# Up projection of the last 1024 tokens as seven products of half blocks, down projection in stages of its own

## The chip, the cores and the metric

The kernel runs on one core of a Trainium2 chip. The metric is device time of one launch in microseconds (us); lower is better. The core has five engines with a queue each: PE multiplies matrices, DVE and ACT work element by element, POOL does small work and issues some DMAs, SP issues most DMAs.

## What is computed

One layer of a hybrid decoder over 2048 tokens of width 1024, float32: a mixer (differential attention, a gated linear recurrence, gated DeltaNet), its output projection and residual, then a gated feed-forward of width 2816 with a causal convolution over three tokens, and a final norm. The part that changes:

```python
h = h + jnp.einsum("bte,ed->btd", mix, w_out[l])

u = rmsnorm(h, ffn_norm_w[l])
up = jnp.einsum("btd,df->btf", u, ffn_w_up[l])
up = causal_depthwise_conv(up, ffn_conv_w[l]) + ffn_conv_b[l].astype(up.dtype)
gate, val = jnp.split(up, 2, axis=-1)
h = h + jnp.einsum("btf,fd->btd", jax.nn.silu(gate) * val, ffn_w_down[l])
return rmsnorm(h, final_norm_w)
```

## The kernel before

Each large product is made of three PE passes: `split` (L89) turns a float32 operand into a high part (a cast on ACT, L92) and a low part (a subtraction on DVE, L93), and `mm3` (L98) adds high x high, high x low and low x high in PSUM, as three matmuls of 128 x 128 by 128 x 512.

`phase_p` projects the input in two halves of 1024 tokens, and runs the recurrences and the attention of the first half beside that. `tail` (L983) does the rest. Its order in the code: the DeltaNet groups of the second half (`dn_half`), then for each 512 tokens (a piece) the output projection and residual (`residual`), the norm with its transposes (`piece_norm`) and the feed-forward (`ffn`). Pieces 0 and 1 run one after the other; beside them the second half's attention (L882) is fed in through `Pump`, a share of its steps after each group. Its memory is that of the DeltaNet groups. Pieces 2 and 3 come last, together, and share each weight load.

`ffn` takes two blocks of 128 features at a time. `ffn_block` loads the gate and the value weights of a block (512 KB each, tile `wu`), splits them, multiplies by the piece's `uh`, `ul` (24 matmuls each), copies PSUM to `raw`, convolves (L1154, L1157) and gates (L1161 to L1163), and splits the gated product into `gh`, `gl`. `down` (L1085) then multiplies the two blocks by their down weights, six matmuls per PSUM bank, and DVE adds each bank to the residual `h` in SBUF (L1098). After the last block `final` scales and stores.

The order on each engine's queue is not that of the code: the code is traced with `tile.TileContext(nc, schedule_with_timeline_sim=True)`, and a planner orders the instructions at build time by their place in the code and when it thinks them ready; buffers of one name and pool are taken in turn, and one that is in use makes its next user wait. A pool that is closed leaves its memory to the next one opened. Each engine then runs its queue in order.

Of the kernel before, what the change touches and what calls it, by code (L numbers as in the profile page):

```python
# [19 lines left out]
P = 128  # L20
# [10 lines left out]
W_BUFS = 3  # L31
D_BUFS = 2
G_BUFS = 3
S_BUFS = 2
T_BUFS = 2
U_BUFS = 1
N_BUFS = 2
# [9 lines left out]
PUMP0 = 0  # L47
PUMP1 = 19
E2_AT = 9
# [34 lines left out]
class K:  # L84
# [13 lines left out]
    def mm3(self, ps, a, b, start, stop):  # L98
        mm = self.nc.tensor.matmul
# [52 lines left out]
    def scratch(self, ctx):  # L152
# [6 lines left out]
        self.s_mix = d.tile([8, P, T], F32, name="s_mix")  # L159

# [290 lines left out]
    def dn_open(self, ctx):  # L451
        tc = self.tc
        self.dw = ctx.enter_context(tc.tile_pool(name="dw", bufs=1))
        self.dps = ctx.enter_context(tc.tile_pool(name="dps", bufs=2, space=PSUM))
# [409 lines left out]
    def att_open(self, ctx, p0_bufs, p1_bufs, s_bufs, t_bufs, slots):  # L864
        tc = self.tc
        self.p_bufs, self.kslots = (p0_bufs, p1_bufs), slots
        self.kq = ctx.enter_context(tc.tile_pool(name="kq", bufs=1))
        self.ap = ctx.enter_context(tc.tile_pool(name="ap", bufs=2))
        self.sm = ctx.enter_context(tc.tile_pool(name="sm", bufs=2))
        self.pss = ctx.enter_context(tc.tile_pool(name="pss", bufs=s_bufs, space=PSUM))  # L870
        self.pst = ctx.enter_context(tc.tile_pool(name="pst", bufs=t_bufs, space=PSUM))
        pso = ctx.enter_context(tc.tile_pool(name="pso", bufs=1, space=PSUM))
# [110 lines left out]
    def tail(self, out):  # L983
        tc, nc, a = self.tc, self.nc, self.a
        with ExitStack() as ctx:
            fc = ctx.enter_context(tc.tile_pool(name="fc", bufs=1))
            self.fw = ctx.enter_context(tc.tile_pool(name="fw", bufs=2))
            self.fps = ctx.enter_context(tc.tile_pool(name="fps", bufs=U_BUFS, space=PSUM))
            self.fpd = ctx.enter_context(tc.tile_pool(name="fpd", bufs=N_BUFS, space=PSUM))
            self.wup = a["ffn_w_up"][0].rearrange("(db p) f -> p db f", p=P)  # L990
            wbc = self.wbc = fc.tile([P, D], F32, name="wbc")
            nc.sync.dma_start(wbc, a["ffn_norm_w"].broadcast_to([P, D]))
            carry = self.carry = fc.tile([P, 2 * NF, 2], F32, name="carry")
            nc.gpsimd.memset(carry, 0.0)
# [229 lines left out]
```

## Time and profile before

| | |
|---|---|
| time, median of 3 runs | 3050.1 us (3049.32 to 3056.87) |
| profiled execution | 3049.23 us, span 3047.5 us |
| PE busy | 2924.1 us, 96% |
| DVE busy | 2087.3 us, 68% |
| ACT busy | 1351.2 us, 44% |
| POOL busy | 315.7 us, 10% |
| mean granted clock of PE | 0.978 |

The span goes from the first to the last instruction of one execution; the rest of its time lies around it. A busy share is the time in which an engine has an instruction under way. PE's instructions overlap each other, so the sum of their durations is longer than its busy time, and a full PE can still be one that waits a little at each matmul. The profile gives the time from the span's start.

### The profile page before, as it was taken

To read this page: it belongs to the slowest core of one execution; us is meant where nothing else is said; L and a number is where in the kernel's file an instruction comes from. 1 tells how busy PE (TensorE), PEld (TensorE's weight loads), DVE (VectorE), ACT (ScalarE), POOL (GpSimd) and SP (SyncE) were. 2 spreads that over 40 slices of the span, in tenths; PEclk is the share of its full clock that TensorE was granted. 3 is DMA by queue.
4 is the path that set the end of the run, shared out by engine and by line. 5 is a ranking of instruction groups with operands and counts; after the bars stand their busy time and mean duration, and the time that the engine had idled before them with its cause. 6 is when DMAs were issued, how large, how long until landed. Compare 5 with 4: busy or idle time off the path is not lost.

```text
span 3047.5 us, 50581 instructions
## 1 busy us (share of the span) xinstructions
PE 2924.1 (96%) x20010; PEld 2384.5 (78%) x20010; DVE 2087.3 (68%) x3923; ACT 1351.2 (44%) x2558; POOL 315.7 (10%) x569
## 2 busy tenths in 40 slices
PE   8999989999998899999899999999799999999998
PEld 6888867777887677877687888887577888888887
DVE  7463775386677877967798888888467555555556
ACT  4222242253455444343666766667235223333323
POOL 1100101021111111202011111110001000000000
PEclk9999979999999999999999999999899999999999
DMA  5336444355646423324524333332313111111111
GB/s 173 94 109 168 129 118 135 91 143 152 183 124 195 103 77 97 90 77 136 158 68 128 100 109 97 101 100 76 100 52 104 49 42 49 56 49 46 52 42 69
DMA packets 373008, 307.88 MB, mean 101 GB/s; under 512 B 65883, under 2 KB 322723, under 8 KB 372771
## 3 DMA queue, kind: packets, MB, share of 16 engines
q1 hardware_dynamic: 333475, 258.51, 28.9%
q0 software_dynamic: 39296, 46.14, 6.2%
q8 instruction: 157, 2.57, 0.4%
q14 instruction: 80, 0.66, 0.1%
HBM read 237.49 MB, written 67.11 MB: 100 GB/s over the span
## 4 chain that ended last, share of the span: by engine, by line
PE 86%; DVE 5%; DMA 3%; ACT 3%; issue 2%; POOL 0%; SPq 0%; POOLq 0%; ACTq 0%; DVEq 0%
PE pp L100 17%; PE pp L101 17%; PE pp L102 17%; PE pd L100 7%; PE pd L102 7%; PE pd L101 7%; PE o L966 4%; PE s L921 4%; PE t L958 2%; PE t L443 1%; PE t L808 1%; DMA wr<-in_ffn_w_down_dram 1%; DVE nb L925 1%; DMA q<-s_q 1%; DMA x<-in_x_dram 1%
## 5 line engine op out<-in xcount | busy, mean ns | idle before, releaser
L100 PE MATMUL pp<-uh,wh 128*128 128x512 f32 x2304 | 916.5, 398 | 12.4 <-ACT raw L1148 9.1
L101 PE MATMUL pp<-ul,wh 128*128 128x512 f32 x2304 | 909.5, 395 | 2.9 <-DVE ul L194 2.9
L102 PE MATMUL pp<-uh,wl 128*128 128x512 f32 x2304 | 906.2, 394 | 0.0
L100 PEld LDWEIGHTS pp<-uh,wh 128*128 128x128 f32 x2304 | 436.2, 189 | 110.7 <-ACT raw L1148 15.4
L101 PEld LDWEIGHTS pp<-ul,wh 128*128 128x128 f32 x2304 | 436.0, 189 | 92.9 <-DVE ul L194 4.6
L102 PEld LDWEIGHTS pp<-uh,wl 128*128 128x128 f32 x2304 | 435.5, 189 | 92.9 <-issue 0.7
L100 PE MATMUL pd<-dh,gh 128*128 128x512 f32 x832 | 332.4, 402 | 15.0 <-ACT gh L92 11.0
L101 PE MATMUL pd<-dl,gh 128*128 128x512 f32 x832 | 329.5, 396 | 0.5 <-DVE dl L93 0.4
L102 PE MATMUL pd<-dh,gl 128*128 128x512 f32 x832 | 324.2, 395 | 0.0
L1098 DVE TENSOR_TENSOR h<-h,pd 128x512 f32<-128x512 f32 x360 | 243.7, 684 | 112.6 <-PE pd L102 111.7
L1157 DVE SCALAR_TENSOR_TENSOR cv<-raw,columns,cv 128x512 f32<-128x512 f32 x352 | 263.9, 750 | 73.7 <-ACT cv L1154 70.0
L927 ACT ACTIVATE p<-s,nb 128x512 f32<-128x512 f32 (+3 forms) x320 | 199.4, 625 | 127.6 <-DVE nb L925 108.7
L925 DVE TENSOR_REDUCE nb<-s 128x1 f32<-128x512 f32 (+3 forms) x320 | 192.5, 608 | 72.2 <-PE s L921 35.8
L93 DVE TENSOR_TENSOR wl<-wu,wh 128x1024 fp32r<-128x1024 f32 x132 | 161.3, 1223 | 71.2 <-ACT wh L92 69.7
L921 PE MATMUL s<-k,q 128*128 128x512 f32 (+3 forms) x640 | 190.3, 388 | 18.3 <-ACT p L927 13.8
L100 PEld LDWEIGHTS pd<-dh,gh 128*128 128x128 f32 x832 | 157.2, 190 | 51.1 <-ACT gh L92 11.5
L92 ACT CAST wh<-wu 128x1024 fp32r<-128x1024 f32 x132 | 138.7, 1051 | 127.2 <-PE pp L101 115.4
L92 ACT CAST gh<-th 128x512 fp32r<-128x512 f32 x120 | 74.1, 619 | 256.6 <-DVE th L1163 182.0
L101 PEld LDWEIGHTS pd<-dl,gh 128*128 128x128 f32 x832 | 157.8, 190 | 34.6 <-DVE dl L93 1.9
L102 PEld LDWEIGHTS pd<-dh,gl 128*128 128x128 f32 x832 | 157.0, 189 | 35.1 <-DVE gl L93 0.4
L92 ACT CAST dh<-wr 128x1024 fp32r<-128x1024 f32 x78 | 80.2, 1051 | 234.9 <-PE pd L102 210.8
L1154 ACT ACTIVATE cv<-raw,columns 128x512 f32<-128x512 f32 x176 | 144.1, 819 | 13.0 <-POOL raw L1149 0.4
(281 smaller groups left out, 4186.5 us busy)
## 6 DMA issues: line engine op xcount, KB each, us to landing
wu<-in_ffn_w_up_dram SPq DMA_DIRECT2D x132, 512.0 KB, 4.0
wr<-in_ffn_w_down_dram SPq DMA_DIRECT2D x66, 512.0 KB, 3.3
wr<-in_w_in_dram SPq DMA_DIRECT2D x56, 512.0 KB, 4.4
q<-s_q POOLq DMA_DIRECT2D x32, 512.0 KB, 5.7
k<-s_k POOLq DMA_DIRECT2D x28, 512.0 KB, 5.4
v<-s_v POOLq DMA_DIRECT2D x28, 512.0 KB, 5.1
wr<-in_w_out_dram SPq DMA_DIRECT2D x24, 512.0 KB, 4.9
x<-in_x_dram SPq DMA_DIRECT2D x16, 512.0 KB, 5.1
```

The lines of the kernel that those rows point to most:

```text
L92: self.nc.scalar.copy(hi, src)
L93: self.nc.vector.tensor_tensor(lo, src, hi.bitcast(F32), op=ALU.subtract)
L100: mm(ps, lhsT=a[0], rhs=b[0], start=start, stop=False)
L101: mm(ps, lhsT=a[0], rhs=b[1], start=False, stop=False)
L102: mm(ps, lhsT=a[1], rhs=b[0], start=False, stop=stop)
L921: nc.tensor.matmul(ps[:, 0:n], lhsT=qS[:, m, i, qs], rhs=kS[c][:, m, 0:n], start=i == 0, stop=i == 1 and not diag)
L925: nc.vector.tensor_reduce(nb[:, c, m:m + 1], ps[:, 0:n], axis=AX.X, op=ALU.max, negate=True)
L927: nc.scalar.activation(t, ps[:, 0:n], AF.Exp, bias=nb[:, c, m:m + 1], accum_out=ls[:, c, m:m + 1])
L966: nc.tensor.matmul(oc[:, 0:256], lhsT=x[:, ks], rhs=vt, start=c == 0 and k == 0 and i == 0, stop=c == len(pd) - 1 and ks.stop == n and i == 1)
L1098: nc.vector.tensor_tensor(h, h, pt, op=ALU.add)
L1154: nc.scalar.activation(c, r[:, 0:512], AF.Identity, bias=self.fcb[:, idx:idx + 1], scale=self.fcw_l[0][:, idx:idx + 1])
L1157: nc.vector.scalar_tensor_tensor(c, r[:, j:j + 512], self.fcw_l[j][:, idx:idx + 1], c, op0=mult, op1=ALU.add)
```

## The change

Pieces 0 and 1 are now normed one after the other and then go through each feature block together, so that a weight block is loaded and split once for both. The gated products aren't split there but written to DRAM (`s_g`), and the residual goes to DRAM too (`s_h`). The down projection is a stage of its own for each 512 tokens and each 512 outputs: its weights and the gated products are loaded and split block by block, all 22 blocks are summed in four PSUM banks, and DVE adds the residual once at the end. The attention of the second half starts after 20 of the 44 block steps and ends with the third of these stages; of its two PSUM banks for transposes one is left, and the feed-forward has four banks in place of three.

For the last 1024 tokens the up projection is a product of 2 x 2 blocks: gate and value by two halves of the 1024 inputs, times two halves of the inputs by two pieces. `forms` makes the seven sums of input blocks in SBUF once, `up7` makes the sums of weight blocks (two on POOL, two on DVE) for each feature block and then seven products where eight stood, adding them up in PSUM and on DVE. A pair of pieces has one convolution and gating of 1024 columns. Their down projection is again four stages, after all up products.

```diff
-T_BUFS = 2
+T_BUFS = 1
+DOWN_LAST = 4
+ATT_AT = 20
...
+        self.s_h = d.tile([T, D], F32, name="s_h")
+        self.s_g = d.tile([NF, P, T], F32, name="s_g")
...
     def tail(self, out):
...
+            main = self.ups = self.dns = Rot((pool(ctx, "fps", bufs=4, space=PSUM), "pp"))
+            ca = ExitStack()
+            with ExitStack() as c1:
+                ux = pool(c1, "ux", bufs=1)
+                self.fw = pool(c1, "fw", bufs=2)
+                with ExitStack() as c2:
+                    self.dn_open(c2, side="right")
+                    self.ct = self.load_consts(self.dw, DN_CONSTS, "dn_consts")
+                    rs = pool(c2, "rs", "right", bufs=1)
+                    self.dn_half(1)
+                    u = []
+                    for s in range(2):
+                        h = [x for i in range(2) for x in rows(slot(ux, 4 + i, F32) if s == 0 else slot(rs, i, F32))]
+                        self.residual([s], [h], rs, 3, 2)
+                        us = [[slot(ux, s * 4 + x * 2 + g) for g in range(2)] for x in range(2)]
+                        self.piece_norm(h, lambda g, cs, pv: self.hi_lo(us[0][g][:, :, cs], us[1][g][:, :, cs], pv))
+                        u.append(us)
+                self.att_open(ca, P0_BUFS, P1_BUFS, S_BUFS, T_BUFS, 4, side="right")
+                att = Pump(self.attention(8, 16), 4 * 100)
+                pump = lambda n: att.upto((n - ATT_AT) / (2 * NF + 3 * 11 - ATT_AT))
+                for f in range(NF):
+                    for s in self.ffn_block(f, u):
+                        pump(2 * f + s + 1)
+            with ExitStack() as c1:
+                self.fw = pool(c1, "fw2", bufs=2)
+                down = self.down([0, 1], out, 1, main)
+                for s, dc, f in down:
+                    n = 2 * s + dc
+                    if n < 3:
+                        pump(2 * NF + n * 11 + f // 2)
+                    if (n, f) == (3, 0):
+                        break
+                att.upto(1)
+                ca.close()
+                uy = pool(ctx, "uy", "right", bufs=1)
+                sl = partial(slot, uy)
+                banks = Rot((pool(ctx, "fps2", "right", bufs=4, space=PSUM), "pp"))
+                self.ups, self.dns = banks, banks
+                hs = [[x for i in p for x in rows(sl(i, F32))] for p in ((8, 10), (9, 12))]
+                self.residual([2, 3], hs, self.fw, 3, 4)
+                B = self.forms(sl, hs)
+                for _ in down:
+                    pass
+            banks.pools += main.pools
+            with ExitStack() as c1:
+                self.fw = pool(c1, "fw3", bufs=2)
+                for f in range(NF):
+                    self.up7(f, B)
+            with ExitStack() as c1:
+                self.fw = pool(c1, "fw4", bufs=2)
+                for _ in self.down([2, 3], out, DOWN_LAST, banks):
+                    pass
...
+    def forms(self, sl, hs):
...
+        b11, b21 = plain(hs[0], 0, 1)
+        b12, b22 = plain(hs[1], 2, 3)
+        done("11", b11, 6, 7)
+        t3 = sub(b22, b12, 4)
+        t1 = sub(b12, b11, 5)
+        t2 = sub(b22, t1, 2)
+        done("T1", t1, 0, 11)
+        done("22", b22, 5, 13)
+        B["T4"] = sl(3), None
+        t4 = []
+        for c in range(2):
+            t4.append(self.fw.tile([P, D], F32, name="t4", tag="wr", bufs=3))
+            nc.vector.tensor_tensor(t4[c], flat(b21, c), flat(t2, c), op=ALU.subtract)
+            nc.scalar.copy(flat(B["T4"][0], c), t4[c])
+        done("21", b21, 8, 9)
+        done("T3", t3, 10, 12)
+        done("T2", t2, 1, 4)
+        B["T4"] = B["T4"][0], sl(2)
+        for c in range(2):
+            h, l = (flat(v, c) for v in B["T4"])
+            nc.vector.tensor_tensor(l, t4[c], h.bitcast(F32), op=ALU.subtract)
+        return B
+    def up7(self, f, B):
+        nc, wk, tt = self.nc, self.fw, self.nc.vector.tensor_tensor
+        raw = []
+        for e in range(2):
+            c0 = e * DFF + f * P
+            raw.append(wk.tile([P, ND, P], F32, name="wu", tag="wr", bufs=3))
+            nc.sync.dma_start(raw[e], self.wup[:, :, c0:c0 + P])
+        wt = lambda: [wk.tile([P, ND, P], F32R, name=n, bufs=4) for n in ("wh", "wl")]
+        lo, up = slice(0, 4), slice(4, 8)
+        w1, w2, w3, w4 = wt(), wt(), wt(), wt()
+        self.split(*w1, raw[0])
+        s = [wk.tile([P, ND, P], F32, name=f"ws{i}", bufs=1) for i in range(2)]
+        nc.gpsimd.tensor_tensor(s[0][:, lo], raw[1][:, lo], raw[1][:, up], op=ALU.add)
+        nc.gpsimd.tensor_tensor(s[1][:, lo], raw[0][:, lo], raw[1][:, lo], op=ALU.subtract)
+        tt(s[0][:, up], s[0][:, lo], raw[0][:, lo], op=ALU.subtract)
+        tt(s[1][:, up], raw[0][:, up], s[0][:, up], op=ALU.subtract)
+        self.split(*w2, s[0])
+        self.split(*w3, s[1])
+        self.split(w4[0][:, up], w4[1][:, up], raw[1][:, up])
+        A = {k: [x[:, r] for x in w] for k, w, r in (
+            ("11", w1, lo), ("12", w1, up), ("S1", w2, lo), ("S2", w2, up), ("S3", w3, lo), ("S4", w3, up), ("22", w4, up))}
+        def prod(ps, x, y, start):
+            for d in range(4):
+                self.mm3(ps, [v[:, d] for v in A[x]], [v[:, d] for v in B[y]], start and d == 0, d == 3, skip=True)
+        def kept(ps, name):
+            t = wk.tile([P, 512], F32, name=name, bufs=1)
+            nc.scalar.copy(t, ps)
+            return t
+        pb, pa, pc = (self.ups.tile([P, 512], F32, name="pp") for _ in range(3))
+        r = [wk.tile([P, 1026], F32, name=f"raw{e}") for e in range(2)]
+        cols = slice(2, 514), slice(514, 1026)
+        prod(pb, "11", "11", True)
+        x1 = kept(pb, "x1")
+        prod(pa, "12", "21", True)
+        tt(r[0][:, cols[0]], x1, pa, op=ALU.add)
+        prod(pb, "S2", "T2", False)
+        x2 = kept(pb, "x2")
+        prod(pc, "S1", "T1", True)
+        x5 = kept(pc, "x5")
+        prod(pb, "S3", "T3", False)
+        tt(r[1][:, cols[1]], x5, pb, op=ALU.add)
+        prod(pc, "S4", "22", False)
+        tt(r[0][:, cols[1]], x2, pc, op=ALU.add)
+        prod(pb, "22", "T4", False)
+        nc.scalar.copy(r[1][:, cols[0]], pb)
+        for e in range(2):
+            nc.gpsimd.tensor_copy(r[e][:, 0:2], self.carry[:, f + e * NF, :])
+        self.glu(f, r, 2, 1024)
+    def glu(self, f, r, s, n):
...
+        nc.sync.dma_start(self.s_g[f, :, s * 512:s * 512 + n], th)
...
+    def down(self, ss, out, nl, banks):
...
+        for s in ss:
+            t0 = s * 512
+            sq = wk.tile([P, 2, 4], F32, name="sq")
+            o = [wk.tile([P, D], F32, name=f"o{tt}", bufs=1) for tt in range(4)]
+            for tt in range(4):
+                nc.sync.dma_start(o[tt], self.s_h[t0 + tt * P:t0 + (tt + 1) * P, :])
+            for dc in range(2):
+                ds = slice(dc * 512, (dc + 1) * 512)
+                pt = [banks.tile([P, 512], F32, name="pd") for _ in range(4)]
+                def load(f):
+                    x = []
+                    for n, src in (("d", a["ffn_w_down"][0, f * P:(f + 1) * P, ds]), ("g", self.s_g[f, :, t0:t0 + 512])):
+                        raw = wk.tile([P, 512], F32, name=f"{n}r", tag="th", bufs=4)
+                        nc.sync.dma_start(raw, src)
+                        x.append([wk.tile([P, 512], F32R, name=n + y, bufs=max(nl + 1, 3)) for y in "hl"])
+                        self.split(*x[-1], raw)
+                    return x
+                def mm(f, x, tt):
+                    (dh, dl), (gh, gl) = x
+                    js = slice(tt * P, (tt + 1) * P)
+                    self.mm3(pt[tt], (gh[:, js], gl[:, js]), (dh, dl), f == 0, f == NF - 1)
+                for f in range(NF - nl):
+                    x = load(f)
+                    for tt in range(4):
+                        mm(f, x, tt)
+                    yield s, dc, f
+                last = [(f, load(f)) for f in range(NF - nl, NF)]
+                for tt in range(4):
+                    for f, x in last:
+                        mm(f, x, tt)
+                    h = o[tt][:, ds]
+                    nc.vector.tensor_tensor(h, h, pt[tt], op=ALU.add)
+                    j = wk.tile([P, 512], F32, name="j", bufs=1)
+                    nc.scalar.activation(j, h, AF.Square, accum_out=sq[:, dc, tt:tt + 1])
+                    if dc == 0:
+                        continue
+                    rs = wk.tile([P, 1], F32, name="rs", bufs=3)
+                    nc.vector.tensor_tensor(rs, sq[:, 0, tt:tt + 1], sq[:, 1, tt:tt + 1], op=ALU.add)
+                    self.rsqrt(rs, rs, 1.0 / D, EPS)
+                    nc.vector.scalar_tensor_tensor(o[tt], o[tt], rs, wfin, op0=ALU.mult, op1=ALU.mult)
+                    r0 = t0 + tt * P
+                    nc.sync.dma_start(out[0, r0:r0 + P, :], o[tt])
```

## Rows read from the trace of the kernel before

**Rows 1.** The page's first part: busy us, share of span, instructions of each engine.
```profile
PE 2924.1 (96%) x20010; PEld 2384.5 (78%) x20010; DVE 2087.3 (68%) x3923; ACT 1351.2 (44%) x2558; POOL 315.7 (10%) x569
```

**Rows 2.** The page's chain that ended last, shares by engine.
```profile
PE 86%; DVE 5%; DMA 3%; ACT 3%; issue 2%; POOL 0%; SPq 0%; POOLq 0%; ACTq 0%; DVEq 0%
```

**Rows 3.** Windows: stretch, length, busy PE PEld DVE ACT POOL, clock, DMA share, GB/s.
```profile
963.00:1100.00 137.00, 121.21 (x723) 95.56 (x724) 118.73 (x220) 60.13 (x99) 19.67 (x28) 0.93 0.42 120
1430.00:1600.00 170.00, 154.93 (x782) 126.43 (x781) 140.31 (x272) 105.46 (x239) 22.25 (x39) 0.96 0.46 133
1437.00:2157.00 720.00, 685.62 (x3582) 571.26 (x3580) 594.56 (x1161) 472.94 (x1074) 92.31 (x171) 0.98 0.37 105
2100.00:2310.00 210.00, 176.65 (x802) 144.22 (x801) 136.56 (x238) 78.62 (x162) 10.66 (x21) 0.90 0.25 78
2310.00:3040.00 730.00, 729.71 (x3185) 597.63 (x3183) 432.02 (x577) 253.47 (x350) 32.82 (x97) 1.00 0.17 53
```

**Rows 4.** Groups by line and form: busy us, mean ns; idle before and its releasers.
```profile
L1157 DVE SCALAR_TENSOR_TENSOR cv<-raw,columns,cv 128x512 f32<-128x512 f32 x352 | 263.9, 750 | 73.7 <-ACT cv L1154 70.0
L1098 DVE TENSOR_TENSOR h<-h,pd 128x512 f32<-128x512 f32 x360 | 243.7, 684 | 112.6 <-PE pd L102 111.7
L93 DVE TENSOR_TENSOR wl<-wu,wh 128x1024 fp32r<-128x1024 f32 x132 | 161.3, 1223 | 71.2 <-ACT wh L92 69.7 <-PE t L958 0.7
...
L92 ACT CAST wh<-wu 128x1024 fp32r<-128x1024 f32 x132 | 138.7, 1051 | 127.2 <-PE pp L101 115.4 <-DMA wu<-in_ffn_w_up_dram 10.9
...
L93 DVE TENSOR_TENSOR gl<-th,gh 128x512 fp32r<-128x512 f32 x120 | 82.8, 690 | 60.8 <-ACT gh L92 58.5 <-PE pd L101 0.8
...
L92 ACT CAST gh<-th 128x512 fp32r<-128x512 f32 x120 | 74.1, 619 | 256.6 <-DVE th L1163 182.0 <-PE pd L101 46.8 <-DMA th<-s_mix 11.3
...
L178 DVE SCALAR_TENSOR_TENSOR u<-h,rs,wbc 128x1024 f32<-128x1024 f32 x12 | 15.4, 1281 | 0.0
...
L597 POOL MEMSET Ld<- 128x512 f32 x4 | 2.1, 525 | 76.2 <-PE t L588 76.2
```

**Rows 5.** Tile carry on POOL: ns min/median/max, first and last start.
```profile
L1149 POOL COPY raw<-carry x132: 174/184/2392, 956.8 to 2988.6; 128x2 f32<-128x2 f32 x132
L1152 POOL COPY carry<-raw x88: 174/753/1432, 1057.1 to 2296.0; 128x2 f32<-128x2 f32 x88
```

**Rows 6.** Timeline of SP's DMA issues, 2600 to 2640: start, us.
```profile
2601.94 0.34 SPq L1080 DMA_DIRECT2D wr<-in_ffn_w_down_dram  x1
```

**Rows 7.** Chain of waits, 2100 to 2310: start, us, what.
```profile
2166.82 3.14 DMA th<-s_mix
2169.98 0.63 ACT gh L92
2170.63 0.70 DVE gl L93
2171.35 3.18 DMA th<-s_mix
```

**Rows 8.** DMA issues: count, KB each, median us from issue to landing.
```profile
q<-s_q POOLq DMA_DIRECT2D x32, 512.0 KB, 5.7
...
th<-s_mix SPq DMA_DIRECT2D x32, 256.0 KB, 3.2
```

**Rows 9.** Windows of tile pp, then of pd: busy PE PEld DVE (ACT).
```profile
1437.00:2157.00 720.00, 269.67 (x1076) 197.19 (x1074) 5.43 (x8) 30.18 (x52) 0.98 0.37 105
...
1437.00:2157.00 720.00, 198.08 (x762) 139.47 (x762) 86.55 (x128) 0.98 0.37 105
```

**Rows 10.** Chain of waits, 1400 to 1620.
```profile
1437.61 16.03 DMA q<-s_q
```

**Rows 11.** Timeline of PE, 2144 to 2320, with idle time before and releaser.
```profile
2166.12 0.80 PE L100 MATMUL pd<-dh,gh 128*128 128x512 f32 x1 [9.68 <-ACT gh L92]
```

**Rows 12.** Chain of waits at the end, 3035 to 3048.
```profile
3039.01 0.60 DVE g L1098
...
3042.58 1.28 DVE u L1122
```

More of the change, by code (lines that the diff above doesn't have):

```diff
@@ L984, in tail @@
         tc, nc, a = self.tc, self.nc, self.a
+        self.wup = a["ffn_w_up"][0].rearrange("(db p) f -> p db f", p=P)
+        pool = lambda c, name, side="left", **kw: c.enter_context(tc.tile_pool(name=name, side=side, reuse_waits="tile", **kw))
+        slot = lambda pl, i, dt=F32R: pl.tile([P, 4, 512], dt, name=f"f{i}")
+        rows = lambda t: [t[:, 2 * i:2 * i + 2].rearrange("p a b -> p (a b)") for i in range(2)]
         with ExitStack() as ctx:
-            fc = ctx.enter_context(tc.tile_pool(name="fc", bufs=1))
@@ L1031, in tail @@
-            for what, g in self.ffn([p2, p3], out):
-                if (what, g) == ("up", 0):
-                    self.final([p1], out)
-            self.final([p2, p3], out, ("wh", "wl", "wr"))
-    def piece(self, s, pool, gp, gb, hn="h"):
-        pc = dict(s=s, pool=pool, gp=gp, gb=gb)
-        pc["h"] = [pool.tile([P, D], F32, name=f"{hn}{i}", bufs=1) for i in range(4)]
-        return pc
-    def residual(self, pcs):
-        nc, a = self.nc, self.a
-        def load():
-            for pc in pcs:
-                for i, h in enumerate(pc["h"]):
-                    r0 = pc["s"] * 512 + i * P
-                    nc.sync.dma_start(h, a["x"][0, r0:r0 + P, :])
+            self.carry = fc.tile([P, 2 * NF, 2], F32, name="carry")
@@ L1052, in residual @@
+    def residual(self, ss, hs, pool, gb, mb):
+        nc, a = self.nc, self.a
+        for s, h in zip(ss, hs):
+            for i, x in enumerate(h):
+                r0 = s * 512 + i * P
+                nc.sync.dma_start(x, a["x"][0, r0:r0 + P, :])
         for e0 in range(0, ND, 2):
-            if e0 == 0 and len(pcs) == 1:
-                load()
             grp = []
@@ L1165, in ffn_block @@
-        return out
+            w.append([wk.tile([P, ND, P], F32R, name=n) for n in ("wh", "wl")])
+            self.split(*w[-1], raw)
+        for s, (uh, ul) in enumerate(us):
+            r = [wk.tile([P, 514], F32, name=f"raw{e}") for e in range(2)]
+            for e in range(2):
+                idx = f + e * NF
+                pt = self.ups.tile([P, 512], F32, name="pp")
+                for d in range(ND):
+                    g, k = divmod(d, 4)
+                    self.mm3(pt, [x[:, d] for x in w[e]], (uh[g][:, k], ul[g][:, k]), d == 0, d == ND - 1)
+                nc.scalar.copy(r[e][:, 2:514], pt)
+                if s == 0:
+                    nc.gpsimd.memset(r[e][:, 0:2], 0.0)
+                else:
+                    nc.gpsimd.tensor_copy(r[e][:, 0:2], self.carry[:, idx, :])
+                nc.gpsimd.tensor_copy(self.carry[:, idx, :], r[e][:, 512:514])
+            self.glu(f, r, s, 512)
+            yield s
```

251 lines of the change are left out of this document (97 added, 154 removed).

## Prediction, made before the result was known

> **What bounds the kernel now.** I read the page's busy line first: the reader is to see TensorE (PE) busy 2924.1 of 3047.5 us, DVE 2087, ACT 1351 [rows 1]. Then the chain of waits: 86% of the span lies on PE, 5% on DVE, 3% on DMA [rows 2]. Then stretches of time, since a mean hides them [rows 3]: from 2310 to 3040, where only the last 1024 tokens' feed-forward runs, PE idles 0.3 us in 730; from 1437 to 2157, where the second half's attention runs beside the feed-forward of the first 1024 tokens, 34 us; from 2100 to 2310, where attention ends and the last pieces start, 33.4 us in 210 at a granted clock of 0.90, so part of it ran at the lower level, 1.2 GHz.
>
> A matmul's duration (some 0.39 us) is no price, since matmuls overlap: the price is the pace. From 2310 to 3040 there are 3185 matmuls, all 128x512, in 730 us: **0.2292 us each** [rows 3].
>
> **The change part by part.** The sum is made against the profiled run, 3049.2 us (span 3047.5 and 1.7 outside); the median shown is 3050.1, 0.9 above.
>
> *Products.* A feature block of the last 1024 tokens took 2 (gate, value) x 2 pieces x 8 x 3 = 96 matmuls; now 7 products x 4 x 3 = 84, of the same shape. 22 x 12 = 264 fewer. The down projection and the residuals keep their number. As PE is the bound in that stretch, 264 x 0.2292 = **-60.5 us**.
>
> *What that stretch asks of DVE instead* (0.3 us of PE idle is its cover). Per block PE takes 84 x 0.2292 = 19.25 us. DVE, by rows 4: three splits of 1024 columns 3 x 1.22, one of 512 0.69, two weight sums 1.38, three adds of products 3 x 0.68, four convolution steps on 1024 columns (0.75 for 512; the other 1024-column operations take 1.28, so some 1.35) 5.4, two gating steps 2 x 1.28: 15.7 us, 82%. ACT: 3 x 1.05 + 0.62 and copies and activations, near 10. DVE ran at 83% from 1437 to 2157 (594.6 of 720) and PE kept on there, so DVE fits. A product that reuses a bank starts one product (2.75 us) after the read that frees it could begin; that read takes 0.7 us, leaving 2 us for queueing behind DVE operations of at most 1.4. The weight slots rotate with some 13 us to spare. I take +2 us, bounds 0 to +60 (the two POOL sums are unpriced: see the second rival).
>
> The POOL sums first as rows show it: a copy of two columns on POOL takes 0.17 us at best, but the one to the carry has a median of 0.75 and a maximum of 1.4, and the one from it goes to 2.4 [rows 5]; 0.75 is the length of a DVE convolution step [rows 4]. So POOL stands still while DVE runs. The Trainium skill, SBUF — State Buffer, section "Who interferes with whom", says that a DVE instruction with two SBUF inputs and a GpSimd instruction that reads SBUF exclude each other for a whole instruction, whichever was first. These copies agree with that for POOL; that DVE is held by POOL no row here shows. By the rule DVE's 15.7 us would grow by both sums' length, by the rows alone it would not.
>
> *Down projection in stages.* Eight stages (512 tokens x 512 outputs), each 22 x 12 = 264 matmuls = 60.5 us if fed. The 320 adds of partial sums to h go (0.68 us of DVE each [rows 4], off the path), 32 stay. New is the feed: per 2.75 us two 256 KB loads (weights, gated products), two casts and two subtractions: DVE 1.38, ACT 1.24, and SP 2 x 0.34 us for issuing [rows 6], all hidden. What decides is the slot cycle: four raw buffers. With such a load a slot's cycle from one DMA's start to the next was 3.14 landing + 0.63 cast + 0.70 subtraction, 4.53 us [rows 7]. Four slots, two loads per f: 2.26 us against PE's 2.75. The cover is gone when landing passes 2 x 2.75 - 1.35 = 4.15 us. The 256 KB load had a median of 3.2; the slow side is 5.7 (q of attention, 512 KB) [rows 8]. But the new rate is 512 KB per 2.75 us, 191 GB/s, and the stretches of rows 3 moved at most 133. Three stages lie beside attention, which lengthens them; five do not (110 f). I take +4, bounds 0 to +86 (landing 5.7: 3.53 us per f, 0.78 x 110).
>
> *Attention denser, with one transpose bank, not two.* From 1437 to 2157 ran 1076 + 762 feed-forward matmuls [rows 9], 421 us, so attention holds some 265 of PE's 685.6 busy us. In the new order it may begin after 20 of 44 up blocks (48 matmuls, 11 us each), but its memory waits for the DeltaNet groups, whose end I leave near 1430, since attention's first load starts at 1437.6 [rows 10]; by then some 27 blocks fit. Left beside it: 17 blocks and 66 f, 1608 matmuls, 369 us: 634 us with attention's own. DVE there: 594.6 less the feed-forward's adds, convolution, gating and splits (some 345) leaves 250; plus 17 x 5.6 and 66 x 1.38 and 8 for adds: 444 of 634, 70%, against 83%. So DVE gets easier. With one bank each of 112 chunks' transposes waits for cast 0.6 and subtraction 0.7 of the chunk before unless other matmuls lie between, which they mostly do. I take +5, bounds 0 to +146 (112 x 1.3).
>
> *Transitions.* 963 to 1100: 15.8 us idle; now a second residual (192 matmuls, 44 us) is ready beside the first norm: -6 (-16 to 0). 1430 to 1600: 15.1 us, where piece 0 ends and piece 1 starts while attention waits for its first q; the two pieces now run together, the q wait stays: -9 (-15 to +5). 2100 to 2310: the largest gap of PE is 9.7 us, from attention's last output through DRAM into the residual [rows 11]. Residual blocks of the early heads can start before that. Then come the norms and the seven sums and their splits: DVE 11 passes of two 1.22 us, 27 us, and eight norm steps of 1.28, of which two of seven products wait for nearly all. Beside them lie 21 f of the fourth down stage, 57 us of matmuls, which want 29 us of DVE themselves. So the idle time mostly moves: -5 (-33 to +25). New are three changes of buffers between stages (up to down, down to up, up to down), where the first loads wait for memory still in use: each costs a landing and a split, 5 us and more, where nothing covers it; attention covers the first. +10 (0 to +30).
>
> *End.* After the last matmul came adds, three 1.28 us scalings and the store [rows 12]; now one half add, one square, one scaling. 0 (-2 to +2).
>
> **Sum:** -60.5 + 2 + 4 + 5 - 6 - 9 - 5 + 10 = -59.5: 2989.7, and against the median **2990 us**.
>
> **The rivals.** (1) *The feed decides* the five bare stages. For it: a rate the trace has not shown and only 0.95 us of spare landing; two loads wait behind each other on in-order queues. Against: the 3.2 us median. At the 5.7 us of rows 8 the stages grow by 86 instead of 4: 3050 - 63.5 + 86 = 3072, slower. It decides from 4.15 us and takes the whole gain from 5.3 ((5.3 + 1.35) / 2 = 3.33 us per f, 0.58 x 110 = 64). (2) *DVE becomes the bound of the seven products.* By rows: 15.7 of 19.25, so it needs 3.5 us more, that is POOL sums that hold DVE for over 1.75 us each. Below, a POOL fill of 512 columns takes 0.53 [rows 4]; no row bounds it above. At 2.6 us each: 22 x 1.7 = 37, 3025. The rule of the skill is what would make this so; without it POOL's time is off the path up to 9.6 us a sum. (3) *One transpose bank or the buffer changes cost more*: a quarter of 112 x 1.3 and the upper end of the swaps, +32 and +20 on top: near 3035. (4) *The idle time goes too*: the tail's transitions hold 64 us and DVE is freer; if 35 more go than I count, 2955. (5) *The saving does not appear*, since the products alternate among three banks: then PE idles in gaps at product ends; 154 products x 0.4 us would be 62 us and 3050. Against it, bank changes after 6 and after 24 matmuls cost nothing from 2310 to 3040 [rows 3].
>
> **How the numbers follow.** Forecast (2965 to 3012) 0.62; idle goes too 0.13; DVE bound 0.08; bank and swaps 0.07; no saving 0.03; feed 0.07. The feed case and half of no saving's mean slower by over 0.3% (9.2 us, about what a measurement here can tell): 0.08; within it, parts of the third and the fifth: 0.06; faster 0.86. The range leaves out the far end of (4) and most of (1): 2955 to 3040; the forecast's own is 2965 to 3012.
>
> **What would show it.** 616 x 3 matmuls in the seven-product stage at 0.229 us and 19.3 us per block; down stages without attention of 61 us each and landings under 4.15; DVE near 82% in the product stage, POOL's sums not on the chain; idle under 35 us between attention's end and the first product. Wrong: down stages over 65 us, a block over 20 us with PE released by DVE, or a gap over 20 us where buffers change.

## The result: slower by 1.3%

The changed kernel took 3089.7 us (median; 3084.1 to 3096.7) beside 3049.7 for the kernel before on the same chip: ratio 1.0128, 95% interval 1.0101 to 1.0154, slower by 40 us. The forecast was 2990. The profiled execution took 3096.7 us, the slowest of the four.

The page's first part after the change (columns as in [rows 1]):

```profile
PE 2913.1 (94%) x19746; PEld 2352.4 (76%) x19746; DVE 2055.0 (66%) x3801; ACT 1426.0 (46%) x2736; POOL 354.5 (11%) x568
```

PE has 264 matmuls fewer, which should take 60 us off its busy time; it lost only 11, its idle time rose from 123 to 182 us, and its mean granted clock fell from 0.978 to 0.967. Where, the windows of the changed kernel show: length, busy PE (and, in the last two, PEld, DVE, ACT, POOL), clock, DMA share, GB/s.

```profile
963.00:1100.00 137.00, 124.02 (x743) 0.95 0.47 144
1250.00:1450.00 200.00, 200.00 (x1427) 1.00 0.23 69
1750.00:1950.00 200.00, 199.37 (x1036) 1.00 0.64 189
1950.00:2160.00 210.00, 166.38 (x859) 0.88 0.24 61
2160.00:2400.00 240.00, 207.85 (x916) 0.94 0.40 124
...
2390.00:2803.00 413.00, 409.15 (x1761) 331.38 (x1759) 326.57 (x315) 193.95 (x231) 84.92 (x79) 1.00 0.23 76
2803.00:3088.00 285.00, 255.06 (x1056) 201.06 (x1056) 138.96 (x216) 114.28 (x207) 3.81 (x7) 0.94 0.62 191
```

The seven products run as forecast: PE 99% busy, DVE 326.6 of 413 us, 79%. The last four down stages take 285 us where 242 were counted: 30 us of that is PE's idle time, and PE is busy for 13 us longer than counted, at a granted clock of 0.94, so part of it ran at the lower level. The largest hole is new: 1950 to 2160, 43.6 us idle at a clock of 0.88, at attention's end. The kernel before idled 17.5 us there, and its largest hole came after attention [rows 3]:

```profile
1950.00:2160.00 210.00, 192.47 (x1015) 0.96 0.31 92
```

The bank maxima `nb` of attention (two for each 512 or fewer columns of scores) show how late it is: length, busy DVE (count), clock, DMA share, GB/s.

```profile
1500.00:1700.00 200.00, 37.65 (x72) 0.99 0.36 101
1700.00:1900.00 200.00, 35.92 (x67) 0.98 0.65 197
1900.00:2050.00 150.00, 38.76 (x77) 0.91 0.44 123
2050.00:2150.00 100.00, 35.42 (x67) 0.88 0.18 45
```

The kernel before did 46 of these from 2050 to 2150, this one 67:

```profile
2050.00:2150.00 100.00, 22.00 (x46) 0.95 0.21 64
```

There attention runs nearly alone in the changed kernel; the down stages' matmuls (tile `pd`) number 60 from 1950 to 2160:

```profile
1950.00:2160.00 210.00, 14.60 (x60) 11.01 (x59) 2.47 (x4) 0.88 0.24 61
```

And it had begun late. Its first load in the timeline of POOL, in the changed kernel and then in the one before:

```profile
1504.87 0.76 POOL L882 DMA_DIRECT2D k<-s_k  x1
...
1431.78 0.76 POOL L886 DMA_DIRECT2D k<-s_k  x1 [4.07 <-DMA wr<-in_ffn_w_down_dram]
```

PE's idle time by releaser from 1430 to 2350 (line, what it waited for, us in total, times, longest). Tile `s` holds scores, `p` their exponentials, which free the bank of `s`; `t` holds the transposes, which a cast (`ph`) and a subtraction (`pl`) free; `o` is the output. Lines are of each run's own kernel. The first line is of the kernel before, the others of the changed one:

```profile
PE s L921 <- ACT p L927: 8.9, 12, 1.6
...
PE s L917 <- ACT p L923: 30.0, 40, 2.8
PE o L973 <- DVE on L972: 11.1, 12, 2.7
PE t L954 <- DVE pl L87: 5.3, 6, 1.5
```

and the two gaps where the buffers change, in PE's timeline, idle time and releaser in brackets (the counterpart of [rows 11]):

```profile
2367.07 0.80 PE L94 MATMUL pp<-f,wh 128*128 128x512 f32 x1 [15.16 <-ACT wh L86]
...
2818.31 2.08 PE L94 MATMUL pd<-dh,gh 128*128 128x512 f32 x4 [19.16 <-ACT gh L86]
```

So there are four suspects: attention and DeltaNet, the sums, the feed of the last stages, the changes of buffers. All times below are medians; each is compared with 3089.7 for the changed kernel, and the ratio is to the kernel before, run beside it (3048.9 to 3051.8). The interval of the changed kernel's own ratio is some 8 us to either side, so 5 us is no difference that can be told, and 9 or 10 us is one only just.

### The profile page after: what moved, and what is told of

It reads as the page before. It is cut to its first block, busy times and chain, and to the rows that moved or that the text cites. A ratio compares the mean times of both kernels' runs of the same rounds, so it can differ in the third digit from the quotient of the medians.

```text
span 3094.9 us, 51350 instructions
## 1 busy us (share of the span) xinstructions
PE 2913.1 (94%) x19746; PEld 2352.4 (76%) x19746; DVE 2055.0 (66%) x3801; ACT 1426.0 (46%) x2736; POOL 354.5 (11%) x568
## 5 line engine op out<-in xcount | busy, mean ns | idle before, releaser
L94 PE MATMUL pp<-f,wh 128*128 128x512 f32 x1320 | 522.6, 396 | 15.2 <-ACT wh L86 15.2
L95 PE MATMUL pp<-f,wh 128*128 128x512 f32 x1320 | 521.0, 395 | 0.0
L96 PE MATMUL pp<-f,wl 128*128 128x512 f32 x1320 | 514.0, 395 | 0.1
L94 PE MATMUL pp<-uh,wh 128*128 128x512 f32 x896 | 358.2, 400 | 0.0
L95 PE MATMUL pp<-ul,wh 128*128 128x512 f32 x896 | 355.2, 397 | 0.0
L96 PE MATMUL pp<-uh,wl 128*128 128x512 f32 x896 | 355.2, 397 | 0.0
L94 PEld LDWEIGHTS pp<-f,wh 128*128 128x128 f32 x1320 | 249.4, 189 | 70.7 <-ACT wh L86 15.6
L96 PEld LDWEIGHTS pp<-f,wl 128*128 128x128 f32 x1320 | 249.1, 189 | 55.5 <-DVE wl L87 0.5
L95 PEld LDWEIGHTS pp<-f,wh 128*128 128x128 f32 x1320 | 249.4, 189 | 54.9 <-issue 0.2
L96 PEld LDWEIGHTS pp<-uh,wl 128*128 128x128 f32 x896 | 169.3, 189 | 35.5 <-issue 0.5
L95 PEld LDWEIGHTS pp<-ul,wh 128*128 128x128 f32 x896 | 169.6, 189 | 34.2 <-DVE ul L190 0.4
L94 PEld LDWEIGHTS pp<-uh,wh 128*128 128x128 f32 x896 | 169.7, 190 | 33.6
```

## Experiments

**The products by themselves.** Eight products, no sums:

```diff
-                B = self.forms(sl, hs)
+                B = []
+                for s in range(2):
+                    us = [[sl(s * 4 + x * 2 + g) for g in range(2)] for x in range(2)]
+                    self.piece_norm(hs[s], lambda g, cs, pv: self.hi_lo(us[0][g][:, :, cs], us[1][g][:, :, cs], pv))
+                    B.append(us)
...
-                    self.up7(f, B)
+                    self.up8(f, B)
...
```

> The changed kernel with the last 1024 tokens' up projection as eight products (96 matmuls a block) and without the seven sums; all else as changed. Theory A (the products saved what was forecast, the loss lies elsewhere): the up stage grows from 418 us to 22 x 96 x 0.2292 = 484 us, the stretch before it gets 5 to 20 us shorter since the sums and their splits go; in all +45 to +60 us, 3135 to 3150. Rival B (seven products gain little because their sums, on POOL and DVE, slow everything): the up stage stays within 25 us of 418, and the kernel comes out at 3080 to 3110.

3138.8 us, ratio 1.0293 (1.0279 to 1.0307): 49 us slower than with seven. Theory A. The saving is real, net of the sums; the changed kernel loses some 89 us elsewhere.

**The feed of the last stages.**

```diff
-raw = wk.tile([P, 512], F32, name=f"{n}r", tag="th", bufs=4)
+raw = wk.tile([P, 512], F32, name=f"{n}r", tag="th", bufs=8 if nl > 1 else 4)
```

> The changed kernel with eight raw buffers in place of four for the last four down stages (2803 to 3088, 285 us for 242 us of matmuls). Theory A (the slot cycle of four buffers paces the feed there): the four stages take 250 to 262 us, the kernel 3062 to 3070. Rival B (the rate of the transfers or the issuing paces it): 280 us or more, the kernel within 6 us of the changed one. Rival C (the idle time is all in the first gap of 19 us at the change of buffers): no change either, with the idle time in the first 25 us.

3071.6 us, ratio 1.0069 (1.0056 to 1.0083): 18 us off, theory A, though 1.6 us outside its range. ACT's idle time in the last stages after the first gap, with four buffers (2822 to 3088):

```profile
ACT gh L86 <- DMA gr<-s_g: 116.8, 68, 4.0
```

and with eight (2822 to 3060):

```profile
ACT gh L86 <- PE pd L95: 89.9, 58, 1.9
...
ACT gh L86 <- DMA gr<-s_g: 10.9, 9, 2.1
```

The releaser changes sides: with four the cast waits for the load, with eight for PE, which is then the bound. From 2822 on PE then needs 242 us for 1051 matmuls and idles 2.4:

```profile
2822.00:3064.00 242.00, 239.61 (x1051) 0.99 0.62 204
```

The median landings were the same within 0.1 us in both kernels, so slots and not the rate were short. DMA issues with four buffers (KB each, median us to landing):

```profile
dr<-in_ffn_w_down_dram SPq DMA_DIRECT2D x84, 256.0 KB, 3.2
gr<-s_g SPq DMA_DIRECT2D x84, 256.0 KB, 3.7
```

**The changes of buffers.** One 4 KB buffer that outlives the stages takes the first weight half and the first down pair; `wfin` and the residual are loaded at f == 4 (and, to make room, `x2` shares `x1`'s buffer and the first stages' `j` lies in PSUM).

```diff
+                self.pf = pool(ctx, "pf", "right", bufs=1)
...
-            raw.append(wk.tile([P, ND, P], F32, name="wu", tag="wr", bufs=3))
+            raw.append(self.pf.tile([P, ND, P], F32, name="wu", tag="pf") if f == 0 and e == 0 else wk.tile([P, ND, P], F32, name="wu", tag="wr", bufs=3))
...
+                    own = self.pf.tile([P, 2, 512], F32, name="pd2", tag="pf") if f == 0 and s == ss[0] and dc == 0 and nl > 1 else None
...
```

> The changed kernel with one 4 KB buffer outside the stages' pools, which takes the first weight half of the seven-product stage and the first pair of loads of the last down stages, so that they can be loaded ahead of the change of buffers; and the loads of the residual and of the final weight are issued after four blocks of the stage, not ahead of its first. Theory A (each change of buffers costs a landing plus a split that nothing covers: gaps of 15.2 and 19.2 us): both gaps shrink by 6 to 12 us, the kernel 3067 to 3079. Rival B (the gaps are set by the sums before the first product and by the last gating before the first down block, not by the loads): gaps within 3 us of 15.2 and 19.2, the kernel within 6 us of the changed one.

3081.0 us, ratio 1.0107 (1.0089 to 1.0125): 9 us off. Both gaps shrank, as theory A had it, to 8.1 us in two parts and 4.1:

```profile
2351.22 0.56 PE L94 MATMUL pp<-f,wh 128*128 128x512 f32 x1 [3.63 <-ACT wh L86]
2357.56 0.80 PE L96 MATMUL pp<-f,wl 128*128 128x512 f32 x1 [4.50 <-DVE wl L87]
...
2795.89 2.08 PE L94 MATMUL pd<-dh,gh 128*128 128x512 f32 x4 [4.08 <-ACT gh L86]
```

but of 22 us closed 9 came through, 2 us short of theory A's range. With both edits:

> The changed kernel with eight raw buffers in the last down stages and with the early loads at the two changes of buffers together; alone they gave 18 and 9 us. Theory A (two costs of their own; in the kernel with early loads alone the four-buffer feed took back what the gap at the last change gave): both gaps under 5 us and the last four stages within 5 us of 242: 18 + 25 us, 3045 to 3053. Rival B (they overlap, since early loads only bring the feed's limit forward): 3062 to 3072.

3066.0 us, ratio 1.0045 (1.0031 to 1.0059): 24 us off. That lies in rival B's range, but the two gains very nearly add: 24 of the 27 that they gave alone.

**How many banks the up products have beside DeltaNet.** Feed-forward matmuls that stand between the steps of DeltaNet or attention in PE's queue are called their company here. The changed kernel's planned order holds 1222 of them between DeltaNet's first and last recurrence step in the tail, that of before 1016. My reading is that with four banks a product is always at hand. With one bank for up products:

```diff
-main = self.ups = self.dns = Rot((pool(ctx, "fps", bufs=4, space=PSUM), "pp"))
+pa, pb = pool(ctx, "fpa", bufs=1, space=PSUM), pool(ctx, "fpb", bufs=3, space=PSUM)
+self.ups, self.dns = Rot((pa, "pp")), Rot((pb, "pp"))
+main = Rot((pa, "pp"), (pb, "pp"), (pb, "pp"), (pb, "pp"))
```

> The changed kernel with its four feed-forward PSUM banks parted: the up products may use one, residual three, the down stages all four. Theory A (with four banks the up blocks were planned so densely between the DeltaNet steps, 1222 feed-forward matmuls against 1016 before, that its end moved from 1427 to 1506, and attention found too little work left beside it): 747 such matmuls are now among DeltaNet's, its end comes at 1400 to 1450, attention has some 2100 feed-forward matmuls beside it and not 1395, the stretch from DeltaNet's end to the first of the seven products loses 30 to 45 us of idle time, the kernel 3045 to 3062. Rival B (attention is slow for its one transpose bank or for DVE, whatever lies beside it): attention's end stays within 15 us of 2157 and the kernel within 10 us of the changed one. Rival C: one bank makes PE wait for each copy of a product out of PSUM (0.6 us of 5.5): slower by 20 us or more.

3084.7 us, ratio 1.0119 (1.0105 to 1.0133): no difference that can be told. Theory A's places came true and its time didn't: DeltaNet ended early, and attention's first load came at 1385.8. Both of rival B's signs came true: attention's end stayed (its last output, tile `mx`, starts at 2181.0 and not 2183.7), and so did the time. PE now idles beside DeltaNet, where it was busy for 146 of 150 and 200 of 200 us (columns: length, busy PE, PEld, DVE, ACT, POOL, clock, DMA share, GB/s; the first line is of the changed kernel):

```profile
1100.00:1250.00 150.00, 146.03 (x1041) 117.00 (x1039) 91.22 (x159) 64.87 (x88) 15.36 (x46) 0.97 0.26 78
...
1100.00:1250.00 150.00, 130.69 (x1180) 102.46 (x1179) 96.56 (x172) 60.22 (x83) 25.14 (x42) 0.91 0.24 76
1250.00:1450.00 200.00, 183.82 (x1233) 143.47 (x1232) 119.55 (x214) 83.95 (x128) 26.03 (x68) 1.00 0.30 86
```

Two edits more (norm transposes on four banks, `ATT_AT = 4`) spread attention evenly:

> The kernel with one bank for the up products (742 feed-forward matmuls among DeltaNet's and not 1222), with two edits more: the norms' transposes may use all four banks, and attention is paced from the fourth block step on, not the twentieth, so that its 2028 matmuls of company lie evenly beside it (224 to 480 in each of its first seven eighths, none in the last). Theory A (in the one-bank kernel the gain at attention's end was lost again to four waits of 2 us at the norm, to attention's slow start and to two eighths of attention alone): 3045 to 3068. Rival B (the work that can be laid beside DeltaNet and attention is too little for both; what one gains the other loses): within 10 us of the one-bank kernel's 3085.

3090.2 us, ratio 1.0125 (1.011 to 1.014): rival B. The late start of attention, which I first took for the cause, is not it: early or late, what one stage wins the other loses.

**The fourth down stage beside attention** (`n < 4`, `+ 4 * 11`, and the break at the stage's end).

> The changed kernel with the fourth down stage (264 matmuls, 60 us) beside attention too, not beside the residual and the sums of the last pieces; attention is paced over four stages and not three. Theory A (attention finds too little feed-forward work beside it: 1395 matmuls, which last through 4.1 of its 8 equal parts): 1635 now, so about one part of eight less runs alone; each part alone loses some 20 us; what the residual and the sums lose without the stage beside them is 5 to 15 us; the kernel 5 to 20 us faster than the changed one, 3070 to 3085. Rival B (the idle time only moves: the sums and norms, some 40 us of DVE, now stand bare): no faster, 3088 to 3115.

3079.9 us, ratio 1.0094 (1.0081 to 1.0108): 10 us off, theory A, only just clear of the noise, and the gap ahead of the first product grew to 22 us.

**All of these together**, on the one-bank kernel:

> All of it: one bank for up products, transposes on four, attention paced from the fourth step over four down stages (2268 matmuls beside attention, none of its eighths bare but the last, with 51), eight raw buffers and early loads. Theory A (the changed kernel's loss is the sum of attention's missing company, the feed and the changes of buffers): 3005 to 3040, faster than the kernel before. Rival B (company is too little whatever its order; only feed and changes count): 3045 to 3062.

3053.9 us, ratio 1.0014 (1.0005 to 1.0022): rival B. Then with one bank up to block 16 only (`if f == 16: self.ups = main`) and the fourth stage halved; the same with the whole stage; and, with the halved stage, four banks throughout and attention again paced from the twentieth step:

> The kernel with all of it, with two edits more: up products have one bank only in the first 16 blocks, beside DeltaNet, and four after that; and the fourth down stage is halved, 11 blocks beside attention and 11 beside the residual and the sums. Theory A (in the kernel with all of it two costs are left that these edits reach: 22 us of waits for the one bank, and 47 us from the residual's end to the first of the seven products, in which nothing lies beside the sums): a third to a half of each goes, 3028 to 3044, faster than before. Rival B (attention, DeltaNet and sums compete for the same work, and what covers one bares another): 3047 to 3062.

> As the last, but with the whole fourth stage beside attention, so that it differs from the kernel with all of it in the banks after block 16 alone. Theory A (the waits for the one bank cost what they show): 8 to 15 us off, 3038 to 3046, and the sums as bare as before. Rival B (the waits are filled by attention's and DeltaNet's own matmuls once they are late anyway): within 5 us of 3054.

> Four banks for all from the start (DeltaNet ends at about 1506 as in the changed kernel), with the eight raw buffers, the early loads and the halved fourth stage. Theory A (company for attention is what one bank buys, worth 15 to 30 us once the sums are covered): 3054 to 3066, at least 12 us slower than the same with one bank in the first 16 blocks. Rival B (DeltaNet loses with one bank what attention wins): within 8 us of that kernel, whatever it takes.

3052.4 (1.0005, 0.9996 to 1.0013), 3063.2 (1.0039, 1.0027 to 1.005) and 3058.9 (1.002, 1.0012 to 1.0029). Rival B in the first and third (the third lies in theory A's range too, but 7 us from the first and not 12), and in the second slower than either theory. Mending what each trace showed last gave no more, which points at attention itself.

**One transpose bank, on the kernel before.** Its only edit is `T_BUFS = 1`; then also `U_BUFS = 2`, so that the up products get the freed bank.

> The kernel before with one PSUM bank for attention's transposes in place of two, the other left unused until attention ends. 1016 feed-forward matmuls among DeltaNet's, as before; beside attention's eighths 348, 185, 265, 311, 289, 314, 136 and 0. Theory A (one bank costs little by itself, as the forecast's +5 had it, but attention takes more matmuls of company for each step and bares its last eighth): +8 to +25 us, 3059 to 3076. Rival B (one bank is the main loss): +40 us or more. Rival C: no difference, within 6 us.

> The same, with the freed bank given to the up products, so that they have two. Now 1203 feed-forward matmuls stand among DeltaNet's (1222 in the changed kernel) and the last three of attention's eighths have none. Theory A (a second up bank lets the order fill DeltaNet so densely that attention is left alone; that, and not the stages or the sums, is what the changed kernel loses before attention's end): DeltaNet ends at 1470 to 1510, attention runs alone at its end, 25 to 45 us slower than with one up bank, 3085 to 3115. Rival B (what DeltaNet takes is not lost but done, so the time comes back): within 10 us of the kernel with one transpose bank and one up bank.

3081.2 us, ratio 1.0106 (1.0093 to 1.0119), 31 us slower than before; and 3096.2, ratio 1.0153 (1.0139 to 1.0166), 15 more. The first lies between theory A's 25 and rival B's 40, the second between A's 25 and B's 10. So the kernel before, without stages, sums or any other part of the change, loses 46 us by two numbers. (`T_BUFS` also sets how many banks the up products get once attention has ended, three before and two here. That costs nothing: from attention's last output to the end both kernels take 891.0 us.) With one bank alone (PE's waits from 1430 to 2350, against 8.9 us in 12 times before):

```profile
PE s L921 <- ACT p L927: 17.2, 23, 2.5
```

and with the second up bank too, attention's first load moves to 1483.8, late as in the changed kernel (1504.9):

```profile
1483.79 0.76 POOL L886 DMA_DIRECT2D k<-s_k  x1 [11.60 <-DVE dl L93]
```

**The same on the changed kernel.** Attention keeps three banks, but scores and transposes take them in turn:

```diff
+        self.pst = self.pss if t_bufs == 0 else ctx.enter_context(pool(name="pst", bufs=t_bufs, space=PSUM))
...
+                ps = self.pss.tile([P, 512], F32, name="s", tag="st")
...
+            pt = self.pst.tile([P, 512], F32, name="t", tag="st")
...
-                self.att_open(ca, P0_BUFS, P1_BUFS, S_BUFS, T_BUFS, 4, side="right")
+                self.att_open(ca, P0_BUFS, P1_BUFS, 3, 0, 4, side="right")
```

> The changed kernel with attention's three PSUM banks (two for scores, one for transposes) taken in turn by both. Theory A (the single transpose bank is the narrow place): attention takes fewer matmuls of company per step, its uncompanied part shrinks from the last 3.9 eighths to the last 3.5, 8 to 20 us off, 3070 to 3082. Rival B (three banks are too few however they are shared): within 6 us of 3090.

3058.7 us, ratio 1.0029 (1.0018 to 1.0041): **31 us off**, more than theory A asked. So three banks are enough when both may take any of them, and it is the transposes' single bank that costs. (Here scores may hold three banks too, and no run on the changed kernel parts the two; the run on the kernel before took the transposes' bank alone.) The path from the bank to the time is not shown: each such edit also lets the planner order the queues anew, and no run parts that from the bank. PE's waits at the transposes themselves (`t` above, 5.3 us for their subtraction) are small; the scores' wait for their exponentials is the one that grows with one bank and that halves here (1430 to 2350):

```profile
PE s L917 <- ACT p L923: 14.0, 28, 1.4
PE t L954 <- ACT p L923: 11.4, 14, 4.4
```

and attention's end, most of which has no company, is faster (`nb`, as above; the first row had 77, the second 67, the third 6):

```profile
1900.00:2050.00 150.00, 44.12 (x86) 0.99 0.48 138
2050.00:2150.00 100.00, 31.82 (x65) 0.90 0.15 38
2150.00:2250.00 100.00, 0.00 (x0) 0.94 0.39 128
```

**The last waits, and a version that beats both.** On the kernel with one bank up to block 16: the first pieces' stores on POOL's queue; and four banks for blocks 0 to 2.

> The mended kernel (one bank to block 16, halved fourth stage, eight raw buffers, early loads), with the output stores of the first pieces on POOL's queue and not ahead of the second weight half on SP's. Theory A (the 15.5 us and 6.9 us ahead of and in the first product are partly this queue): 5 to 10 us off, 3042 to 3048. Rival B (the sums on DVE end last anyway): within 4 us of 3052.

> The same with four banks for the first three blocks too, which lie ahead of most of DeltaNet's steps. Theory A (waits for the one bank, and the norm, cost some 10 us there): 3 to 8 us faster than with one bank. Rival B (one competes with the other, as in the kernels so far): within 4 us or slower.

3054.8 us (1.0017, 1.0009 to 1.0026), rival B; 3047.0 (0.9991, 0.9979 to 1.0002), theory A, level with before. Then the shared three banks on that kernel, and on one with four feed-forward banks throughout:

> The best mended kernel (one bank for up products in blocks 3 to 15, halved fourth stage, eight raw buffers, early loads, stores on POOL's queue) with the same sharing of three banks. Theory A: 5 to 15 us off 3047, 3032 to 3042, faster than before. Rival B: within 5 us of 3047.

> The changed kernel with attention's three banks shared, eight raw buffers and early loads, the first pieces' output stores on POOL's queue and the halved fourth stage; four banks for all feed-forward work, as changed. Theory A (costs add up: 31 for the transposes, 24 for feed and changes, 7 for the halved stage as the kernels with four banks showed): 3024 to 3036, the best of all. Rival B (one bank beside DeltaNet is worth something of its own): 3040 to 3052, no better than the one-bank kernel's 3041.

3040.8 us, ratio 0.997 (0.9959 to 0.998), and **3037.5 us, ratio 0.9957 (0.9944 to 0.9971)**: faster than both kernels, by 13 us and 52 us. One bank beside DeltaNet, with the early pacing that goes with it, buys nothing once attention shares its banks. The last lies between the two theories, 1.5 us outside A's range: the single costs add up to 62, and 52 came off.

## Why the prediction was wrong

*Products, -60.5*: right. One run puts seven against eight at 49 us, net of the sums. Whether the sums are the 11 between, no run took by itself.

*DVE and POOL in that stretch, +2*: right, 79% against a forecast 82%. The products themselves run 6 us behind the pace (below). Of the second rival, the operations on DVE were longer than by rows 4 (last section), but DVE had room for that.

*Attention denser, with one transpose bank, +5*: **the step that failed**. One edit on the kernel before gives +31, one edit on the changed kernel takes 31 back. I argued that other matmuls mostly lie between one chunk's transposes and the next; spread evenly, the price was 0.28 us for each of 112 chunks, a fifth of the 1.3 us that a cast and a subtraction take. The third rival, with "a quarter of 112 x 1.3", had the size by a guess, not the path: the waits show at the scores, not at the transposes. (Its own sum was off too: 2990 + 32 + 20 is 3042, not 3035.) The step's other assumption, that DeltaNet ends near 1430, was off by some 70 us, and so attention had 1395 matmuls of company in the planned order and not 1608, and in the trace 60 of it from 1950 on; but the one-bank runs show that the end of DeltaNet by itself is worth little. The first load of attention before was k at 1431.8, not q at 1437.6; that changes nothing here.

*Down feed, +4*: mis-sized, 18. The 2.26 us per block was worked out with a landing of 3.14 us, and by the threshold of 4.15 median landings of 3.2 and 3.7 us should have been safe. What makes the cycle longer is argued, not shown: loads, casts and subtractions wait for each other in order on three queues, and four slots hold two blocks, so there is no slack for a late one. The first rival had the feed right and named a too high landing as its condition.

*Three buffer changes, +10*: mis-sized if the gaps are counted: 15.2 and 19.2 us are 34 together, above the bound of 30. Of 22 us closed, 9 came through alone and 6 beside the eight buffers; what the rest costs, no run shows.

*Transitions, -6, -9, -5*: 963 to 1100 idles 13.0 us where 9.8 were counted. 1450 to 1600 has no idle time at all, better than forecast, since attention had hardly begun (its first load is at 1504.9); the hole from 1950 to 2160 is larger than what that saved. After attention, 32 us of idle time from 2160 to 2400 against 33.4 [rows 3]; 15 of it is the gap where buffers change. The 33.4 took in attention's end, and counted from 1950 idle time without that gap grew from 34 to 61 us. Nearly all of the growth lies ahead of attention's end; behind it, from 2160, 16 us before and 17 now, "mostly moves" was right. That the withheld fourth stage costs 10 us stood in no term.

Together: -49 + 31 + 18 + 6 + 10 = +16, against +40 measured. The other 24 us are **open**: the second up bank cost 15 on the kernel before, but giving up three banks brought no more than 5 on the changed one. The best kernel, too, is 13 us ahead of before and not 49.

Where time is lost, a count of matmuls in the profiled runs shows; these are 47 us apart, not 40. First the stretch from 963 to attention's last output (length, busy PE, clock, DMA share, GB/s) before, with one transpose bank on the kernel before, changed, changed with three shared banks, and in the best kernel:

```profile
963.00:2156.48 1193.48, 1139.02 (x6803) 0.98 0.36 102
963.00:2187.46 1224.46, 1153.10 (x6806) 0.97 0.35 100
963.00:2183.71 1220.71, 1141.83 (x6695) 0.96 0.36 108
963.00:2156.11 1193.11, 1128.23 (x6695) 0.98 0.37 111
...
963.00:2171.84 1208.84, 1146.55 (x6808) 0.98 0.38 113
```

The changed kernel takes 27 us longer and does 108 matmuls less, which are 25 us at 0.2292: 52 us lost. Idle time is 24 of that. The rest is PE busy for longer, at a lower granted clock: a hole costs more than its idle time. Shared banks give 28 back, and 24 stay. Then the last 1060 matmuls, which hold the last four stages, before, changed, with eight buffers and early loads, and in the best kernel:

```profile
2796.68:3047.47 250.79, 243.03 (x1061) 0.99 0.16 54
2798.06:3094.91 296.85, 256.15 (x1061) 0.94 0.60 188
2799.93:3063.50 263.57, 246.44 (x1061) 0.97 0.64 210
...
2768.95:3031.96 263.01, 244.92 (x1061) 0.97 0.64 210
```

They lost 46 us; the two edits give 33 back, and 13 stay. Between the two stretches 10 us are lost, 6 of them in the products. The best kernel still loses 14 us ahead of attention's last output, some 19 between that and the last 1060 matmuls, and 12 in these; what causes them, no run shows.

## What to carry over

A buffer taken from a stage that runs beside others must be priced by taking that one buffer from the kernel as it is; "mostly covered" was wrong by 26 us here, and sharing the remaining ones gave it back. Count a feed's slots with room for a late load, not with the median: four slots at 2.26 us per block against 2.75 lost 18 us, and with eight PE idled 2.4 us in 242. And company is a fixed sum here: what one dependent chain gets beside it, the next one misses, so moving it about gained little.

## What was not expected of the hardware

DVE is held by POOL. Both weight sums on DVE are of one shape; the groups by line from 2390 to 2803 (busy, mean ns):

```profile
L1170 DVE TENSOR_TENSOR ws<-wu,ws 128x512 f32<-128x512 f32 x20 | 32.4, 1618 | 0.0
...
L1169 DVE TENSOR_TENSOR ws<-ws,wu 128x512 f32<-128x512 f32 x19 | 13.1, 692 | 8.5 <-POOL ws L1167 8.5
```

The second waits for the POOL sum ahead of it and takes 0.69 us. The first mostly starts while a POOL sum runs, and takes 1.62 on average: some 1.78 us in the 17 of its 22 records that start under a POOL sum, each of which ends 0.55 us after that sum, and 0.68 to 0.69 in the others:

```profile
L1170 DVE TENSOR_TENSOR ws<-wu,ws x22: 678/1782/1789, 2371.2 to 2763.9; 128x512 f32<-128x512 f32 x22
```

In one pair DVE comes first, at 2412.49: it takes 0.68 us, and the POOL sum, 1.27 us at its shortest, takes 1.76. One of the usual pairs in the timelines: the POOL sum from 2606.94 to 2609.22, DVE's from 2607.99 to 2609.78, 0.56 after the other's end.

```profile
2606.94 2.28 POOL L1168 TENSOR_TENSOR ws<-wu 128x512 f32<-128x512 f32 x1 [4.68 <-DVE wl L87]
...
2607.99 1.79 DVE L1170 TENSOR_TENSOR ws<-wu,ws 128x512 f32<-128x512 f32 x1
```

The Trainium skill, SBUF — State Buffer, section "Who interferes with whom", has it that such instructions exclude each other for a whole instruction; these rows agree, for the side that no row of before showed. It cost some 17 x 1.1 us of DVE's time, which had room.
